# Eight weight buffers with a layout of their own each, and two raw buffers in place of three

## The chip, the cores and the metric

The kernel runs on one core of one Trainium2 chip. The metric is the device time of one execution in microseconds (us).

## The reference

One inference step of a two-layer decoder, for a prompt of 256 positions and a group of 8 x 8 new positions, together T = 320 columns. Layer 0 mixes by gated linear attention (GLA), layer 1 by a gated MLP over chunks of 128 positions (gMLP); each layer ends in a dense MLP with a squared ReLU. All is float32. Cut to what matters here:

```python
proj = x @ w_in                                  # GLA: 2048 x 6144 (and 16 columns for the gate)
o, s_fin = gla_chunked(q, k, v, log_a, s0)
h = (head_norm(o) * silu(r)) @ w_out             # 2048 x 2048
z = gelu(x @ sg_w_in + b)                        # gMLP: 2048 x 4096
h = (u * spatial(layer_norm(v))) @ sg_w_out      # 2048 x 2048
x = layer_norm(alpha * x + h)
x = layer_norm(alpha * x + square(relu(x @ w1)) @ w2)   # 2048 x 8192 and back, in each layer
```

The weights are some 390 MB, each read once; nearly all the work is these products with 320 columns.

## The kernel before

**Products.** A float32 product is made of three products of TensorE's fast type `F32R`: every operand is split into a high part (the cast to `F32R`) and a low part (what is left). `mm3` issues, for one tile of 128 x 128 weights, low weights x high activations (L161), high x low (L162) and high x high (L163), all into one PSUM tile. Activations stand as tiles of 16 rows of 320 columns (`xh`/`xl`, `yh`/`yl`, `hh`/`hl`, `oh`/`ol`); in three places rows have 322 columns (`dgh`/`dgl`).

**Units.** Weights come in units of 128 x 4 x 256 numbers (512 KB): `unit()` takes a raw buffer from the pool `wraw`, issues one transfer on SP's queue (L138), casts it on ScalarE (ACT) into a high buffer `wh` (L144), and subtracts on VectorE (DVE) into a low buffer `wl` (L145). The first unit goes in single rows and the second in pairs. `group()` then lets TensorE (PE) use the unit: two halves of 128 columns (`n`), four rows (`kk`), three matmuls each, 24 in all. The rows of the product are summed over 16 values of `k`, four units (`q`) after each other.

**Buffers.** `wraw` has three buffers. A `Ring` has four high and four low buffers of 4 x 256 numbers, 4096 bytes a partition; between the two sets stands one gap of 64 bytes, so that low buffers begin 64 bytes further in a 256-byte block than high ones. Ring a is there from the start. Ring b is added in `second_half()`, when the GLA's own tiles are given back; from then on units take turns between the rings. Activation tiles begin 128 bytes into a 256-byte block (`LINE // 2`), and a row of 320 numbers is five such blocks.

**Order.** The program is written unit by unit; a `Side` places steps of other work (gates, attention, norms) between units. The tile framework adds all waits from the use of buffers, and its scheduler sets the order on each engine from its own estimate of times, so a change of buffers can move instructions.

**Start.** The first 16 rows of x, the gate's weights (`wgr`, L293 and L296) and the first units all come over SP's queue (x rows by L225, the first two by ACT's). `low_gate()` multiplies them in 32 matmuls (`wgp`, L316 and L317).

Of the kernel before, what the change touches and what calls it, by code (L numbers as in the profile page):

```python
# [8 lines left out]
F32 = mybir.dt.float32  # L9
F32R = mybir.dt.float32r  # L10
# [5 lines left out]
P = 128  # L16
D = 2048
KT = D // P
# [12 lines left out]
UK = 4  # L31
UN = 256
NU = KT // UK
WARM = 9
LINE = 64
# [6 lines left out]
V_N = 216  # L42


class Ring:


    def __init__(self, pool, tag):
        self.pool, self.tag, self.gap = pool, tag, False

    def part(self, p, name):

        t = self.pool.tile([P, UK, UN], F32R, tag=p + self.tag, name=name)
        if not self.gap:
            self.pool.tile([P, LINE // 4], F32, tag="gap", name=name + "_gap", bufs=1)
            self.gap = True
        return t


class Side:  # L60
# [17 lines left out]
def step_kernel(ctx: ExitStack, tc: tile.TileContext, A):  # L78
    nc = tc.nc
    uid = [0]  # L80

    def nm(s):
        uid[0] += 1
        return f"{s}_{uid[0]}"
# [1 line left out]

    cp = ctx.enter_context(tc.tile_pool(name="cp", bufs=1))
    big = ctx.enter_context(tc.tile_pool(name="big", bufs=1))
    wraw = ctx.enter_context(tc.tile_pool(name="wraw", bufs=3))
    wa = ctx.enter_context(tc.tile_pool(name="wa", bufs=4))  # L90
    mm = ctx.enter_context(tc.tile_pool(name="mm", bufs=4, space=bass.MemoryType.PSUM))
    gls = ExitStack()
# [8 lines left out]
    def mmtile(n=T):  # L101

        if mx is not None:
            banks[0] = (banks[0] + 1) % 6
        return (mx if banks[0] > 3 else mm).tile([P, n], F32, tag="mm", name=nm("mm"), padded_shape=[P, 512])
# [19 lines left out]
    def col(c):  # L125
        return vec[:, c : c + 1]


    def unit(w, row0, q, col0, ring):

        raw = wraw.tile([P, UK, UN], F32, tag="raw", name=nm("raw"))
        src = w[row0 // (UK * P) + q, col0 // UN]
        hi = ring.part("h", nm("wh"))
        lo = ring.part("l", nm("wl"))
        units[0] += 1
        step = 2 if units[0] <= 2 else UK
        for k in range(0, UK, step):
            nc.sync.dma_start(raw[:, k : k + step, :], src[:, k : k + step, :])  # L138
        step = 1 if units[0] == 1 else step
        for k in range(0, UK, step):  # L140
            ks = slice(k, k + step)
            if units[0] == 1:
                before_unit(k)
            nc.scalar.copy(hi[:, ks, :], raw[:, ks, :])  # L144
            nc.vector.tensor_sub(lo[:, ks, :], raw[:, ks, :], hi[:, ks, :].bitcast(F32))  # L145
        return hi, lo

    def warm_up():

# [4 lines left out]
    def next_ring():  # L154
        turn[0] += 1
        return rings[turn[0] % len(rings)]

    def mm3(ps, wh, wl, kk, n, rh, rl, k, c0, cn, first, last):
        s = slice(n * P, (n + 1) * P)
        x_h, x_l = rh[:, k, c0 : c0 + cn], rl[:, k, c0 : c0 + cn]  # L160
        nc.tensor.matmul(ps, wl[:, kk, s], x_h, start=first, stop=False)  # L161
        nc.tensor.matmul(ps, wh[:, kk, s], x_l, start=False, stop=False)  # L162
        nc.tensor.matmul(ps, wh[:, kk, s], x_h, start=False, stop=last)  # L163

    def group(w, row0, cols, rh, rl, evict, side=None, width=T, before=None):

        ps = [mmtile(width) for _ in range(2 * len(cols))]
        for q in range(NU):
            if before is not None:
                before(q)  # L170
            for i, c in enumerate(cols):
                wh, wl = unit(w, row0, q, c, next_ring())
                for n in range(2):
                    for kk in range(UK):
                        k = q * UK + kk
                        mm3(ps[2 * i + n][:], wh, wl, kk, n, rh, rl, k, 0, width, k == 0, k == KT - 1)
                if side is not None:
                    side()
        for n in range(2 * len(cols)):
            evict(n, ps[n])  # L180
# [11 lines left out]
    lp = l2 = z = None  # L192
# [5 lines left out]
    def bigtile(tag, dt, name, width=T):  # L198

        t = (lp if tag == "b1" else big).tile([P, BIG], dt, tag=tag, name=nm(name))
        start = LINE // 2 if width == T else 0
        return t[:, start : start + KT * width].rearrange("p (k t) -> p k t", t=width)

    def parts(pair, name, width=T):
        return bigtile(pair + "0", F32R, name + "h", width), bigtile(pair + "1", F32R, name + "l", width)
# [30 lines left out]
    def before_unit(k):  # L239

        x_parts(slice(k, k + 1), first_x[k // 2][:, k % 2 : k % 2 + 1, 0:T])
# [9 lines left out]
    for c0, w in ((0, W0), (W0, W1)):  # L251
        nc.gpsimd.affine_select(out=mf[:, c0 : c0 + w], in_=mf[:, c0 : c0 + w], compare_op=ALU.is_ge, fill=0.0,
                                base=0, pattern=[[1, w]], channel_multiplier=-1)
# [89 lines left out]
    class Head:  # L343


        def __init__(hd, h):
            hd.h = h
            hd.eb, hd.ei, hd.ee = {}, {}, {}
# [140 lines left out]
        def project_kq(hd, side):  # L489

            h = hd.h

            def ev(n, ps):
                if n == 0:
                    side.flush()
                (hd.ev_k if n < 2 else hd.ev_q)(n % 2, ps)

            group(w_in, 0, (C_K + h * DK, C_Q + h * DK), xh, xl, ev, side)

        def project_v(hd, side):  # L500

            c = C_V + hd.h * DV
            hd.vb, hd.vst = {}, []

            def ev(n, ps):
                if n == 2:
                    if hd.h:
                        side.flush()
                    hd.tiles()
                    hd.gather_v(0)  # L510
                hd.ev_v(n, ps)
                if n == 3:
                    hd.gather_v(1)

            if hd.h == 0:
                group(w_in, 0, (c, c + UN), xh, xl, ev, side)
            else:
                for v0 in (0, 2):
                    group(w_in, 0, (c + v0 * P,), xh, xl, lambda n, ps, v0=v0: ev(v0 + n, ps), side)
# [175 lines left out]
    def split_o(ks):  # L695
        for k in ks:
            nc.scalar.copy(oh[:, k, 0:T], o_all[:, k, 0:T])
            nc.vector.tensor_sub(ol[:, k, 0:T], o_all[:, k, 0:T], oh[:, k, 0:T].bitcast(F32))

    def second_half():  # L700

        nonlocal lp, l2, z, gl, mx
        side.flush()
        split_o(range(4 * (H - 1), 4 * H))
        gst.close()
        gls.close()
        gl = ctx.enter_context(tc.tile_pool(name="gs", bufs=2, space=bass.MemoryType.PSUM))
        mx = ctx.enter_context(tc.tile_pool(name="mx", bufs=2, space=bass.MemoryType.PSUM))
        banks[0] = 3
        lp = ctx.enter_context(tc.tile_pool(name="lp", bufs=1))  # L710
        l2 = ctx.enter_context(tc.tile_pool(name="l2", bufs=2))
        wb = ctx.enter_context(tc.tile_pool(name="wb", bufs=4))
        rings.append(Ring(wb, "b"))
        wb.tile([P, LINE // 4], F32, tag="fill", name="fill_b", bufs=1)
        z = lp.tile([P, KT, T], F32, tag="z", name="z")
        lp.tile([P, 3 * LINE // 4], F32, tag="fill", name="fill_l")
        for q in range(2):
            nc.gpsimd.dma_start(z[:, 8 * q : 8 * q + 8, :], xT[:, 8 * q : 8 * q + 8, :])

# [194 lines left out]
    def before(q):  # L914
        if q == NU - 1:
            second_half()
        else:
            split_o(range(UK * q, UK * (q + 1)))
# [131 lines left out]
    ps = {}  # L1050
# [23 lines left out]
    for j in range(KT):  # L1074
        y, g, b = z[:, j, :], col(norm.vg + j), col(norm.vb + j)
# [4 lines left out]
        else:  # L1080
            if j not in ps:
                put_d(j)
            t = l2.tile([P, T], F32, tag="t", name=nm("t"), bufs=3)
# [70 lines left out]
```

## Time and profile before

| | |
|---|---|
| median of 2 runs | 2691.05 us (2690.93 to 2691.17) |
| profiled execution, span from the first to the last instruction | 2689.4 us |
| granted TensorE clock, mean | 1.000 |
| matmuls (PE) | 18,395, 2680.7 us busy |
| DVE / ACT / POOL busy | 1550.3 / 1162.5 / 226.4 us |
| read from memory / written | 409.60 / 22.02 MB |

The profiled execution has no time of its own beside its span; the median of the runs is 1.65 us above that span. In rows of groups, the columns are: line, engine, operation, output<-inputs, shapes, xcount | busy us, mean ns of one | idle time of the engine just before them and what ended it. In rows of the timeline they are: start us, length us, engine, line, operation. In rows of waits: who waited <- for whom: us in total, times, longest us. PEld is TensorE loading weights, SPq SP's queue of transfers. A matmul's length contains its way through the array and overlaps with the next one; the distance between two starts is what each adds to the time.

### The profile page before, as it was taken

What the parts mean: (1) busy time and instruction counts of PE and PEld (TensorE: products, weight loads), DVE (VectorE), ACT (ScalarE), POOL (GpSimd) and SP (SyncE); (2) the same over time, 40 slices, a digit from 0 to 9 for tenths busy, and PEclk for the clock granted to TensorE, in tenths of its full rate; (3) what the DMA queues carried; (4) which work ended last, traced back from release to release, by engine and by line L of the source; (5) the groups of instructions that cost most, each with busy time, mean ns of one, the idle gap of its engine ahead of it and who ended that gap; (6) DMA issues with size and microseconds to landing.
All of it is one profiled execution on the core that took longest, in us unless ns stands there. A gap on an engine that the chain in (4) does not pass through costs nothing.

```text
span 2689.4 us, 44906 instructions
## 1 busy us (share of the span) xinstructions
PE 2680.7 (100%) x18395; PEld 2658.8 (99%) x18395; DVE 1550.3 (58%) x2322; ACT 1162.5 (43%) x1638; POOL 226.4 (8%) x391
## 2 busy tenths in 40 slices
PE   9999999999999999999999999999999999999999
PEld 9999999999999999999999999999999999999998
DVE  7677677885444444444478776686444444444446
ACT  5455455564334334333446554355334333333434
POOL 4353341000000000000001032000000000000000
PEclk9999999999999999999999999999999999999999
DMA  8667667545445545444445555455445444454552
GB/s 252 220 196 249 217 198 253 189 142 159 155 150 155 151 150 156 150 153 152 150 152 161 157 158 149 134 165 153 153 150 156 150 152 154 150 155 150 152 154 79
DMA packets 138494, 442.42 MB, mean 165 GB/s; under 512 B 20912, under 2 KB 27952, under 8 KB 138288
## 3 DMA queue, kind: packets, MB, share of 16 engines
q1 hardware_dynamic: 121440, 408.08, 49.2%
q0 software_dynamic: 16304, 30.82, 3.7%
q8 instruction: 144, 2.36, 0.4%
q10 hardware_dynamic: 544, 0.66, 0.1%
q14 instruction: 62, 0.51, 0.1%
HBM read 409.60 MB, written 22.02 MB: 160 GB/s over the span
## 4 chain that ended last, share of the span: by engine, by line
PE 99%; DMA 0%; ACT 0%; DVE 0%; ACTq 0%; issue 0%; DVEq 0%
PE mm L161 32%; PE mm L163 32%; PE mm L162 31%; PE gl L631 1%; PE gl L634 1%; PE gl L589 1%; PE gl L1003 0%; PE gl L573 0%; DMA raw<-gla_w_in 0%; ACT z L1087 0%; DMA xr<-xT 0%; PE gl L558 0%; PE gl L603 0%; PE gl L574 0%; PE gl L552 0%; PE gl L1004 0%
## 5 line engine op out<-in xcount | busy, mean ns | idle before, releaser
L145 DVE TENSOR_TENSOR wl<-raw,wh 128x1024 fp32r<-128x1024 f32 (+1 forms) x740 | 902.3, 1220 | 953.2 <-ACT wh L144 950.9
L144 ACT CAST wh<-raw 128x1024 fp32r<-128x1024 f32 (+1 forms) x740 | 771.5, 1044 | 1251.9 <-PE mm L163 1127.1
L163 PE MATMUL mm<-yh,wh 128*128 128x320 f32 x2624 | 805.9, 307 | 0.0
L161 PE MATMUL mm<-yh,wl 128*128 128x320 f32 x2624 | 803.2, 309 | 0.0
L162 PE MATMUL mm<-yl,wh 128*128 128x320 f32 x2624 | 794.9, 303 | 0.0
L161 PE MATMUL mm<-hh,wl 128*128 128x320 f32 x2048 | 631.5, 308 | 0.0
L163 PE MATMUL mm<-hh,wh 128*128 128x320 f32 x2048 | 629.0, 307 | 0.0
L162 PE MATMUL mm<-hl,wh 128*128 128x320 f32 x2048 | 619.9, 303 | 0.0
L162 PEld LDWEIGHTS mm<-yl,wh 128*128 128x128 f32 x2624 | 492.7, 188 | 0.0
L163 PEld LDWEIGHTS mm<-yh,wh 128*128 128x128 f32 x2624 | 491.4, 187 | 0.0
L161 PEld LDWEIGHTS mm<-yh,wl 128*128 128x128 f32 x2624 | 491.0, 188 | 0.0
L161 PEld LDWEIGHTS mm<-hh,wl 128*128 128x128 f32 x2048 | 384.6, 188 | 0.0
L162 PEld LDWEIGHTS mm<-hl,wh 128*128 128x128 f32 x2048 | 384.6, 188 | 0.0
L163 PEld LDWEIGHTS mm<-hh,wh 128*128 128x128 f32 x2048 | 383.4, 187 | 0.0
L161 PE MATMUL mm<-xh,wl 128*128 128x320 f32 x768 | 238.2, 311 | 1.4 <-DVE wl L145 0.7
L163 PE MATMUL mm<-xh,wh 128*128 128x320 f32 x768 | 236.4, 309 | 0.0
L162 PE MATMUL mm<-xl,wh 128*128 128x320 f32 x768 | 235.2, 306 | 0.0
L161 PEld LDWEIGHTS mm<-xh,wl 128*128 128x128 f32 x768 | 144.1, 188 | 5.4 <-DVE wl L145 1.0
L162 PEld LDWEIGHTS mm<-xl,wh 128*128 128x128 f32 x768 | 144.3, 188 | 4.4 <-issue 1.2
L163 PEld LDWEIGHTS mm<-xh,wh 128*128 128x128 f32 x768 | 143.7, 187 | 2.6 <-issue 0.7
L1053 POOL CAST ident_r<-ident 128x128 fp32r<-128x128 f32 x1 | 0.3, 286 | 1027.9 <-PE gl L772 1027.9
L936 POOL DMA_DIRECT2D bsp<-sg_wT x1 | 0.6, 558 | 999.7 <-PE mm L163 999.7
(265 smaller groups left out, 2380.3 us busy)
## 6 DMA issues: line engine op xcount, KB each, us to landing
raw<-mlp_w SPq DMA_DIRECT2D x512, 512.0 KB, 3.5
raw<-gla_w_in SPq DMA_DIRECT2D x94, 512.0 KB, 4.1
raw<-sg_w_in SPq DMA_DIRECT2D x64, 512.0 KB, 3.6
st<-state SPq DMA_DIRECT2D x32, 512.0 KB, 5.7
o_state_s<-st POOLq DMA_DIRECT2D x32, 512.0 KB, 4.2
raw<-gla_w_out SPq DMA_DIRECT2D x32, 512.0 KB, 4.5
raw<-sg_w_out SPq DMA_DIRECT2D x32, 512.0 KB, 3.5
va<-blk POOLq DMA_DIRECT2D x128, 32.0 KB, 4.3
```

Of the source, the lines that this page charges most:

```text
L144: nc.scalar.copy(hi[:, ks, :], raw[:, ks, :])
L145: nc.vector.tensor_sub(lo[:, ks, :], raw[:, ks, :], hi[:, ks, :].bitcast(F32))
L161: nc.tensor.matmul(ps, wl[:, kk, s], x_h, start=first, stop=False)
L162: nc.tensor.matmul(ps, wh[:, kk, s], x_l, start=False, stop=False)
L163: nc.tensor.matmul(ps, wh[:, kk, s], x_h, start=False, stop=last)
L589: nc.tensor.matmul(pairs(pu), hd.ktp[:, kt, blk, :], hd.v_prompt(blk), start=(blk == 0), stop=(blk == 1))
L631: nc.tensor.matmul(po[:], qm[:, kt, b * P : (b + 1) * P], part[:], start=False, stop=(b == DB - 1 and kt == 1 and part is sth))
L634: nc.tensor.matmul(pairs(pu), kz[:, i, kt, g, :], hd.v_sample(g), start=True, stop=True)
L936: nc.gpsimd.dma_start(wsT, A["sg_wT"])
L1053: nc.gpsimd.tensor_copy(ident_r[:], ident[:])
```

## The change

A class `Weights` maps row `k` of a unit to its place in a buffer: `base + k // 2 * a + k % 2 * b`. Buffers grow by 256 bytes to 4352, seventeen blocks of 256, and the gap between the sets goes, so that all buffers begin on a block. A table `PLACES` gives each of a ring's four turns a place for high and one for low weights and an order of rows, 1 or -1. `Q` is 64 bytes, `UN` one row of 1024 bytes:

- ring a, turn 0: rows as before, low 64 bytes further in the block than high; turn 1: each row 64 bytes further than the one before it; turn 2: the same places, with `kk` running from 3 to 0; turn 3: rows stand in the order 0, 2, 1, 3, rows 1 and 3 shifted by 128 bytes.
- ring b: rows as before; high and low begin at 0 and 0, 0 and 128, 128 and 192, 64 and 0 bytes in the block.

The sixteen longer buffers take 4096 bytes more in all, as much as the third raw buffer, which goes. Casts and subtractions write rows in pairs with steps `a` and `b`. The first matmul of a sum is now the first in the unit's order of rows.

```diff
+class Weights:
+    def row(self, k):
+        return self.base + k // 2 * self.a + k % 2 * self.b
+    def put(self, ks):
+        k, n = ks.start, ks.stop - ks.start
+        if n == 1:
+            return self.tile[:, self.row(k) : self.row(k) + UN].rearrange("p (a b n) -> p a b n", a=1, b=1)
+        one = self.tile[:, self.row(k) : self.row(k) + 1]
+        return bass.AP(tensor=one.tensor, offset=one.offset,
+                       ap=[list(one.ap[0]), [self.a, n // 2], [self.b, 2], [1, UN]])
...
+Q = LINE // 4
+PLACES = {
+    "a": [((0, 2 * UN, UN), (Q, 2 * UN, UN), 1),
+          ((0, 2 * UN + 2 * Q, UN + Q), (Q, 2 * UN + 2 * Q, UN + Q), 1),
+          ((0, 2 * UN + 2 * Q, UN + Q), (Q, 2 * UN + 2 * Q, UN + Q), -1),
+          ((0, UN, 2 * UN + 2 * Q), (Q, UN, 2 * UN + 2 * Q), 1)],
+    "b": [((0, 2 * UN, UN), (0, 2 * UN, UN), 1),
+          ((0, 2 * UN, UN), (2 * Q, 2 * UN, UN), 1),
+          ((2 * Q, 2 * UN, UN), (3 * Q, 2 * UN, UN), 1),
+          ((Q, 2 * UN, UN), (0, 2 * UN, UN), 1)],
+}
 class Ring:
-        self.pool, self.tag, self.gap = pool, tag, False
-    def part(self, p, name):
-        t = self.pool.tile([P, UK, UN], F32R, tag=p + self.tag, name=name)
...
+    def parts(self, hi, lo):
+        *at, order = PLACES[self.tag][self.turn % 4]
+        self.turn += 1
+        h, l = (Weights(self.pool.tile([P, UK * UN + LINE], F32R, tag=p + self.tag, name=n), *x)
+                for p, n, x in zip("hl", (hi, lo), at))
+        return h, l, order
...
-    wraw = ctx.enter_context(tc.tile_pool(name="wraw", bufs=3))
+    wraw = ctx.enter_context(tc.tile_pool(name="wraw", bufs=2))
...
-            nc.scalar.copy(hi[:, ks, :], raw[:, ks, :])
-            nc.vector.tensor_sub(lo[:, ks, :], raw[:, ks, :], hi[:, ks, :].bitcast(F32))
-        return hi, lo
+            src = raw[:, ks, :].rearrange("p (a b) n -> p a b n", b=min(step, 2))
+            nc.scalar.copy(hi.put(ks), src)
+            nc.vector.tensor_sub(lo.put(ks), src, hi.put(ks).bitcast(F32))
+        return hi, lo, range(UK)[::order]
...
-                    for kk in range(UK):
+                    for kk in order:
...
-                        mm3(ps[2 * i + n][:], wh, wl, kk, n, rh, rl, k, 0, width, k == 0, k == KT - 1)
+                        mm3(ps[2 * i + n][:], wh, wl, kk, n, rh, rl, k, 0, width,
+                            q == 0 and kk == order[0], q == NU - 1 and kk == order[-1])
```

The order changes most where the program starts. On SP's queue, before, from the first transfers on (`raw` are units of weights, `xr` rows of x, `wgr` the gate's weights):

```order
L138 DMA raw_155<-gla_w_in 128x512 x2
L138 DMA raw_201<-gla_w_in 128x512 x2
L225 DMA xr_234<-xT 128x2x320
L225 DMA xr_236<-xT 128x2x320
L138 DMA raw_242<-gla_w_in 128x1024
L293 DMA wgr<-gla_w_low 128x256
L225 DMA xr_302<-xT 128x2x320
L138 DMA raw_272<-gla_w_in 128x1024
```

The same place on SP's queue after the change:

```order
L172 DMA raw_155<-gla_w_in 128x512 x2
L172 DMA raw_200<-gla_w_in 128x512 x2
L261 DMA xr_233<-xT 128x2x320
L261 DMA xr_235<-xT 128x2x320
L329 DMA wgr<-gla_w_low 128x256
L332 DMA wgr_340<-gla_w_gate 16x1024
L261 DMA xr_301<-xT 128x2x320
L172 DMA raw_241<-gla_w_in 128x1024
```

The third unit's transfer (`raw_242`, now `raw_241`) has moved behind three others: its buffer is now the first unit's.

On ACT, before, from the second unit's cast on (`wh` high weights, `xh` high part of x, `wgp` the gate's weights):

```order
L144 CAST wh_202<-raw_201 128x512 x2
L230 CAST xh_89<-xr_234 128x640
L230 CAST xh_89<-xr_236 128x640
L144 CAST wh_243<-raw_242 128x1024
L230 CAST xh_89<-xr_302 128x640
L144 CAST wh_273<-raw_272 128x1024
L230 CAST xh_89<-xr_304 128x640
L310 CAST wgp_418<-wgr 128x8x3x16
```

The same place on ACT after the change:

```order
L179 CAST wh_201<-raw_200 128x2x256 x2
L266 CAST xh_89<-xr_233 128x640
L266 CAST xh_89<-xr_235 128x640
L266 CAST xh_89<-xr_301 128x640
L179 CAST wh_242<-raw_241 128x4x256
L266 CAST xh_89<-xr_303 128x640
L346 CAST wgp_417<-wgr 128x8x3x16
L179 CAST wh_272<-raw_271 128x2x2x256
```

The third unit's cast stands behind one more cast of x and the fourth's behind the gate's weights, and the casts write four rows with steps of their own (`128x2x2x256`, or `128x4x256` where the steps are equal) in place of one run of 1024. On PE, gate matmuls (`wgp`) stand between the third and fourth and the fourth and fifth units; before, the first sixteen followed the fourth unit.

More of the change, by code (lines that the diff above doesn't have):

```diff
@@ L42, with __init__, __getitem__ @@
 V_N = 216
+class Weights:
+    def __init__(self, tile, base, a, b):
+        self.tile, self.base, self.a, self.b = tile, base, a, b
+    def row(self, k):
[7 more added lines that the diff above has]
+                       ap=[list(one.ap[0]), [self.a, n // 2], [self.b, 2], [1, UN]])
+    def __getitem__(self, at):
+        p, k, c = at
+        return self.tile[p, self.row(k) + c.start : self.row(k) + c.stop]
+Q = LINE // 4
[9 more added lines that the diff above has]
+}
 class Ring:
     def __init__(self, pool, tag):
-        self.pool, self.tag, self.gap = pool, tag, False
-    def part(self, p, name):
-        t = self.pool.tile([P, UK, UN], F32R, tag=p + self.tag, name=name)
[L54 to L57, printed above, removed]
+        self.pool, self.tag, self.turn = pool, tag, 0
+    def parts(self, hi, lo):
[4 more added lines that the diff above has]
+        return h, l, order
 class Side:
@@ L132, in unit @@
         src = w[row0 // (UK * P) + q, col0 // UN]
-        hi = ring.part("h", nm("wh"))
-        lo = ring.part("l", nm("wl"))
+        hi, lo, order = ring.parts(nm("wh"), nm("wl"))
         units[0] += 1
@@ L171, in group @@
             for i, c in enumerate(cols):
-                wh, wl = unit(w, row0, q, c, next_ring())
+                wh, wl, order = unit(w, row0, q, c, next_ring())
                 for n in range(2):
-                    for kk in range(UK):
+                    for kk in order:
                         k = q * UK + kk
-                        mm3(ps[2 * i + n][:], wh, wl, kk, n, rh, rl, k, 0, width, k == 0, k == KT - 1)
+                        mm3(ps[2 * i + n][:], wh, wl, kk, n, rh, rl, k, 0, width,
+                            q == 0 and kk == order[0], q == NU - 1 and kk == order[-1])
                 if side is not None:
@@ L715, in second_half @@
         z = lp.tile([P, KT, T], F32, tag="z", name="z")
-        lp.tile([P, 3 * LINE // 4], F32, tag="fill", name="fill_l")
+        lp.tile([P, LINE], F32, tag="fill", name="fill_l")
         for q in range(2):
```

## The prediction

> **What bounds the kernel now.** I began with the page's shares of busy time and its chain, because the change touches TensorE's weights, the two engines that make them and the transfers that feed those, and only one of these can set the end.
>
> ```profile
> PE 2680.7 (100%) x18395; PEld 2658.8 (99%) x18395; DVE 1550.3 (58%) x2322; ACT 1162.5 (43%) x1638; POOL 226.4 (8%) x391
> PEclk9999999999999999999999999999999999999999
> PE 99%; DMA 0%; ACT 0%; DVE 0%; ACTq 0%; issue 0%; DVEq 0%
> PE mm L161 32%; PE mm L163 32%; PE mm L162 31%; PE gl L631 1%; PE gl L634 1%; PE gl L589 1%; PE gl L1003 0%; PE gl L573 0%; DMA raw<-gla_w_in 0%; ACT z L1087 0%; DMA xr<-xT 0%; PE gl L558 0%; PE gl L603 0%; PE gl L574 0%; PE gl L552 0%; PE gl L1004 0%
> ```
>
> TensorE is never without work, its clock is full in every slice, and 99% of the chain is matmuls, nearly all from the three lines of `mm3`. So two things count: how far apart one matmul starts after the other, and whether TensorE ever has to wait for weights. A matmul's recorded length tells neither, since matmuls overlap. I therefore read start times. This is one unit of weights (24 matmuls) in the first MLP, from the timeline of PE; the columns are start, length, engine, line:
>
> ```profile
> 1149.73 0.31 PE L161 MATMUL mm<-hh,wl 128*128 128x320 f32 x1
> 1149.88 0.30 PE L162 MATMUL mm<-hl,wh 128*128 128x320 f32 x1
> 1150.02 0.31 PE L163 MATMUL mm<-hh,wh 128*128 128x320 f32 x1
> 1150.17 0.31 PE L161 MATMUL mm<-hh,wl 128*128 128x320 f32 x1
> ...
> 1153.20 0.31 PE L161 MATMUL mm<-hh,wl 128*128 128x320 f32 x1
> ```
>
> From 1149.73 to 1153.20 there are 24 starts: 3.47 us a unit, **0.1446 us a matmul**. Within a triple the steps are not alike: 0.15 after the first, 0.14 after the second, 0.15 after the third. Same shape, same engine, full clock, so something other than the arithmetic adds to some of them.
>
> Here the rows carry a tile's place in memory. The activation rows are 320 columns, 1280 bytes, five whole blocks of 256; a weight row is 1024 bytes, four blocks; the low weights stand 64 bytes further in their block than the high ones. So before the change every matmul of `mm3` of this width meets the same places. Two stretches have other places:
>
> ```profile
> 545.16 0.30 PE L161 MATMUL mm<-dgh,wl 128*128 128x322 f32 x1
> 545.31 0.31 PE L162 MATMUL mm<-dgl,wh 128*128 128x322 f32 x1
> ...
> 573.52 0.31 PE L163 MATMUL mm<-dgh,wh 128*128 128x322 f32 x1
> 573.68 0.31 PE L161 MATMUL mm<-dgh,wl 128*128 128x322 f32 x1
> ...
> 574.12 0.31 PE L161 MATMUL mm<-yh,wl 128*128 128x320 f32 x1
> L161 PE MATMUL mm<-dgh,wl 128*128 128x322 f32 x192 | 59.6, 311 | 0.0
> L163 PE MATMUL mm<-dgh,wh 128*128 128x322 f32 x192 | 59.6, 310 | 0.0
> L162 PE MATMUL mm<-dgl,wh 128*128 128x322 f32 x192 | 59.4, 309 | 0.0
> ```
>
> ```profile
> 2676.31 0.31 PE L1084 MATMUL mm<-nl,ident_r 128*128 128x320 f32 x1
> ...
> 2677.93 0.31 PE L1085 MATMUL mm<-nh,ident_r 128*128 128x320 f32 x1
> ```
>
> In the first, activation rows are 322 wide, so each row starts 8 bytes further in its block. The three groups hold 192 matmuls a line in three such stretches, so one stretch is 192, and four others of the trace stand among them: 28.96 us for 196, 0.1478 each, or 0.1468 when scaled by 320/322. Single steps there reach 0.16 (573.52 to 573.68). In the second, one stationary tile is loaded again and again: 1.62 us for 11 steps, 0.1473. **So places cost something, and two stretches with other places than the kernel's are both slower, by 0.0022 and 0.0027 us a matmul.**
>
> **The matmuls after the change.** The lines of `mm3` have 5,888 matmuls each (2,624 + 2,048 + 768 + 256 + 192 by group), 17,664 together. Of eight buffers one, the first of ring a, keeps today's places; the units go round the buffers evenly, so 7/8, 15,456 matmuls, get new ones: rows shifted by 64 bytes from one to the next, the same with the four rows taken backwards, rows alternating by 128, and in ring b low and high at equal places, 128 apart, or 64 apart elsewhere in the block. None of these stands in the trace. Bounds from its rows: if each step were the shortest one seen (0.140, rounded as 1149.88 to 1150.02), 15,456 x -0.0046 = -71 us; if each were as in the stretch of 322 columns, 15,456 x 0.0022 = +34 us; as in the last stretch, 15,456 x 0.0027 = +42 us; the single steps of 0.16 are no mean of anything, and I leave them out. I take +0.0016, two thirds of the way to the two slow stretches, since these include offsets of 8 bytes that the new layouts lack: **+25 us**. It lies nearest to the 322-column row, the only one with many places.
>
> The Trainium skill, SBUF — State Buffer, section "Who interferes with whom", gives TensorE two independent read ports, one for the moving operand and one for the weights, and says that it waits for nobody. By that, places would be worth nothing and this term would be 0; the trace's unequal steps of one shape speak against it, and the sum above does not use it.
>
> **The weights' supply with two raw buffers.** In steady state, each transfer is issued by SP when VectorE has finished with the raw buffer it overwrites:
>
> ```profile
> 1117.65 7.26 SPq L138 DMA_DIRECT2D raw<-mlp_w  x3
> 1116.40 1.22 DVE L145 TENSOR_TENSOR wl<-raw,wh 128x1024 fp32r<-128x1024 f32 x1 [0.64 <-ACT wh L144]
> 1118.78 1.05 ACT L144 CAST wh<-raw 128x1024 fp32r<-128x1024 f32 x1 [2.41 <-PE mm L163]
> 1125.71 1.05 ACT L144 CAST wh<-raw 128x1024 fp32r<-128x1024 f32 x1 [2.41 <-PE mm L163]
> raw<-mlp_w SPq DMA_DIRECT2D x512, 512.0 KB, 3.5
> SPq L138 <- DVE wl L145: 2150.6, 692, 8.9
> ACT wh L144 <- PE mm L163: 1127.1, 514, 3.8
> ```
>
> The subtraction ends at 1117.62, the transfer starts at 1117.65 and lands after 3.5, and its cast comes at 1125.71, having waited for TensorE to free a weight buffer, as 514 casts do. With two buffers the transfer for the cast at 1125.71 starts after the subtraction that follows the cast at 1118.78: 1118.78 + 1.05 + 0.03 + 1.22 + 0.03 = 1121.11, landing at 1124.61, still 1.1 us early. So steady state loses nothing. Casts and subtractions now write four separate rows. The nearest rows of that kind are the first unit's single rows, quoted with the start below: 0.71 for two casts, 0.76 for two subtractions. Between no change and the price of four single ones, a cast costs up to 4 x 0.36 - 1.05 = 0.4 us more and a subtraction up to 4 x 0.38 - 1.22 = 0.3. I take 0: one instruction with a longer pattern is nearer to one long instruction than to four. ACT is busy for 43% and DVE for 58%, so TensorE covers it either way; the 1.1 us of the loop would shrink to 0.4. If that cover too is gone, a unit is late by the rest, first drawn from the stock of ready buffers (eight, or four in the mixer's first projections).
>
> At the start there is no cover. The rows are the chain and ACT, DVE and SP at that time:
>
> ```profile
> 4.97 6.32 DMA raw<-gla_w_in
> 11.31 1.07 ACT wh L144
> 12.40 1.24 DVE wl L145
> 13.68 0.42 PE mm L161
> 4.31 0.71 ACT L144 CAST wh<-raw 128x256 fp32r<-128x256 f32 x2 [1.22 <-DMA raw<-gla_w_in]
> 6.28 0.76 DVE L145 TENSOR_TENSOR wl<-raw,wh 128x256 fp32r<-128x256 f32 x2
> 7.06 0.33 SPq L138 DMA_DIRECT2D raw<-gla_w_in  x1
> 14.25 1.05 ACT L144 CAST wh<-raw 128x1024 fp32r<-128x1024 f32 x1 [0.98 <-DMA raw<-gla_w_in]
> raw<-gla_w_in SPq DMA_DIRECT2D x94, 512.0 KB, 4.1
> st<-state SPq DMA_DIRECT2D x32, 512.0 KB, 5.7
> ```
>
> The third unit's transfer goes out at 4.97 into a third buffer, and TensorE waits for it. With two it waits for the first unit's last subtraction, which ends at 7.04, the time at which the fourth goes out today (7.06, cast at 14.25). So the third cast moves from 11.31 to about 14.25: **+2.9 us**. Behind it, units come at half the loop: (6.3 + 1.06 + 1.23) / 2 = 4.3 us while transfers take 6.3, against 3.47 of matmuls; the thirteen gate matmuls that the new order puts ahead of the fourth and fifth unit (13 x 0.147 = 1.9 us) fill part of that. I add 2 us, between 0 and (4.3 - 3.47) x 8 units = 7. What is queued on SP behind a waiting raw transfer waits too: the gate weights, the x rows and later the state loads; their readers are the side steps, which TensorE runs between units.
>
> The accumulation flags now follow the order of the rows and cost nothing.
>
> **Sum:** the profiled execution's span 2689.4 + 25 + 2.9 + 2 = 2719.3. The median of the runs, 2691.05, lies 1.65 above that span, so the time is **2721 us**, +1.1%. The bound for telling it from no change is about 2% (54 us).
>
> **Rivals.**
> - *Places do not matter, or the seven cancel.* For it: one old layout out of many may be typical. Against: unequal steps in the rows. The layout term is 0: 2691 + 5 = 2696. This is also where the skill's rule of separate ports leads.
> - *The new places are faster (the other side).* Before the change one step in three is short. If the new places give two short ones, a triple loses 0.007 us: 15,456 / 3 x -0.007 = -36 us, with the start 2660. It decides as soon as the seven together save more than the start's 5 us, a mean step under 0.1443. For it: 0.14 does occur in the rows; against: neither stretch with other places has a mean under 0.1468.
> - *Two raw buffers starve the mixer's part.* There the median landing is 4.1, and with a state load's 5.7 the loop is (5.7 + 1.05 + 1.22) / 2 = 4.0 us, 0.5 over 3.47. For half of its 94 units that is 25 us on top: 2746. Against: half the loop at 4.1 is 3.2, under 3.47.
>
> **How the numbers follow.** Forecast 0.60 (2700 to 2745), no effect of places 0.14, faster places 0.14, starvation 0.12. The range 2686 to 2752 takes in the two slow stretches' 34 and 42 us with the start's 10 and the starvation's 2746 above, and no effect or a small saving below; it leaves out most of the faster case and the end of the others. Over 2% faster (under 2637) needs nearly the whole -71: 0.03. Over 2% slower (above 2745): 0.12. Within: 0.85.
>
> **What would show it.** Starts of one unit's 24 matmuls, buffer by buffer: the buffer with the old places keeps 3.47 us, the others differ, each the same every time it comes round; ring b's first, with low and high alike, should be about 3.53, as with the one tile loaded again and again. TensorE's third unit should start near 16.6 instead of 13.7, and later waits of TensorE should stay at nothing. The forecast is wrong if units with new places run under 3.46 on average, or if the casts' waits turn from TensorE to transfers and TensorE shows gaps.

## The result, and the profile after

The changed kernel takes **2724.74 us** (median of 2 runs, 2724.38 to 2725.11), against 2691.05: 33.7 us more, a ratio of 1.0125 with a 95% interval from 1.0095 to 1.0154. The forecast was 2721 with a range of 2686 to 2752. The profiled execution has a span of 2722.7, 33.3 us over that of before.

The page of the changed kernel, its busy times, clock, chain and two groups of supply instructions:

```profile
PE 2705.7 (99%) x18395; PEld 2680.9 (98%) x18395; DVE 1550.4 (57%) x2322; ACT 1161.1 (43%) x1638; POOL 226.7 (8%) x391
PEclk9999999999999999999999999999999999999999
PE 78%; DVE 3%; DMA 3%; ACT 1%; issue 0%; ACTq 0%; POOL 0%; DVEq 0%; POOLq 0%
L180 DVE TENSOR_TENSOR wl<-raw,wh 128x1024 fp32r<-128x1024 f32 (+1 forms) x740 | 901.1, 1218 | 986.2 <-ACT wh L179 984.3
L179 ACT CAST wh<-raw 128x1024 fp32r<-128x1024 f32 (+1 forms) x740 | 771.7, 1043 | 1280.2 <-PE mm L198 997.4
```

The matmuls are as many and the clock is full. But the chain is no longer TensorE alone: transfers, casts and subtractions enter it with some 7% of the span. The fall of TensorE's share from 99% to 78% is mostly another thing: the profile could follow this chain back only to 421.85 us, so its shares add up to 85% and not to 100%. The casts and subtractions themselves cost what they did, 1043 and 1218 ns now, 1044 and 1220 before, although ring a's turns 1 to 3 now write four separate rows.

**Where the units' time went.** The starts of units in the same MLP as in the prediction, from the timeline of PE of the changed kernel (start, length, engine, line), one row for the first matmul of a unit; units alternate between ring b and ring a:

```profile
1155.40 0.31 PE L196 MATMUL mm<-hh,wl 128*128 128x320 f32 x1
...
1158.92 0.31 PE L196 MATMUL mm<-hh,wl 128*128 128x320 f32 x1
...
1162.39 0.31 PE L196 MATMUL mm<-hh,wl 128*128 128x320 f32 x1
...
1165.89 0.31 PE L196 MATMUL mm<-hh,wl 128*128 128x320 f32 x1
...
1169.38 0.31 PE L196 MATMUL mm<-hh,wl 128*128 128x320 f32 x1
...
1172.90 0.31 PE L196 MATMUL mm<-hh,wl 128*128 128x320 f32 x1
...
1176.39 0.31 PE L196 MATMUL mm<-hh,wl 128*128 128x320 f32 x1
...
1179.91 0.31 PE L196 MATMUL mm<-hh,wl 128*128 128x320 f32 x1
...
1183.41 0.31 PE L196 MATMUL mm<-hh,wl 128*128 128x320 f32 x1
```

The distances are 3.52 (ring b, 128 and 192), 3.47 (ring a, the old place), 3.50 (b, 64 and 0), 3.49 (a, rows shifted by 64 each), 3.52 (b, 0 and 0), 3.49 (a, the same backwards), 3.52 (b, 0 and 128) and 3.50 (a, rows shifted by 128). The round of eight takes 28.01 us, where eight old units take 27.73 (1146.27 to 1174.00 in the timeline of before). The old place keeps its 3.47, and all seven others are slower, each by 0.02 to 0.05 us every time it comes round. Of the 736 units (17,664 / 24) the first 102 know ring a alone, whose four places are 0.02 us above the old one on average. So the units give 634 x 0.28 / 8 + 102 x 0.02 = 24 us. Over the whole trace, the mean step between the starts of neighbouring `mm3` matmuls, leaving out steps from 0.2 us on, went from 144.66 to 145.93 ns: 17,664 x 1.27 ns = **22.4 us**.

**The rest is waits.** These are the rows of PE's and ACT's waits after (waiter <- for whom: us in total, times, longest):

```profile
PE mm L196 <- DVE wl L180: 3.6, 2, 3.2
PE mm L196 <- DVE nw L223: 2.3, 1, 2.3
...
PE mm L197 <- DVE yl L858: 1.0, 1, 1.0
...
ACT wh L179 <- PE mm L198: 997.4, 440, 4.9
ACT wh L179 <- DMA raw<-mlp_w: 113.0, 67, 5.6
```

Before, casts waited 24.4 us for `mlp_w`, as its rows of waits have it:

```profile
ACT wh L144 <- DMA raw<-mlp_w: 24.4, 12, 3.7
```

So some casts did turn from waiting for TensorE to waiting for transfers, and TensorE has gaps. I add up what each distance between neighbouring matmul starts above 0.31 us has over a normal step of 0.147, by stretch of the span:

| us lost in gaps | 0–20 | 20–445 | 445–560 | 560–620 | 620 to the end | all |
|---|---|---|---|---|---|---|
| before | 1.9 | 11.6 | 0.2 | 0.0 | 0.4 | 14.1 |
| after | 4.2 | 15.4 | 3.3 | 1.2 | 0.4 | 24.5 |
| `before_raw2` (below) | 3.6 | 15.9 | 2.2 | 5.5 | 0.4 | 27.6 |
| `old_places` (below) | 3.4 | 15.5 | 2.9 | 4.1 | 0.4 | 26.3 |
| `halves4` (below) | 1.8 | 14.2 | 1.8 | 0.0 | 0.4 | 18.2 |

After minus before is **10.4 us**. With the 22.4 of the places this makes 32.8 of the 33.3 us between the spans. Nothing more is lost in the dense MLP of layer 0 and after it, beyond 620 us, which is more than three quarters of the span.

### The profile page after: what moved, and what is told of

Same layout as the page of the kernel before. It is cut to its first block, busy times and chain, and to the rows that moved or that the text cites. A ratio compares the mean times of both kernels' runs of the same rounds, so it can differ in the third digit from the quotient of the medians.

```text
span 2722.7 us, 44866 instructions
## 1 busy us (share of the span) xinstructions
PE 2705.7 (99%) x18395; PEld 2680.9 (98%) x18395; DVE 1550.4 (57%) x2322; ACT 1161.1 (43%) x1638; POOL 226.7 (8%) x391
## 4 chain that ended last, share of the span: by engine, by line
PE 78%; DVE 3%; DMA 3%; ACT 1%; issue 0%; ACTq 0%; POOL 0%; DVEq 0%; POOLq 0%
PE mm L196 26%; PE mm L198 26%; PE mm L197 26%; DMA raw<-gla_w_out 2%; DVE wl L180 1%; ACT wh L179 1%; DMA raw<-mlp_w 1%; DMA z<-xT 0%; PE gl L1039 0%; ACT z L1123 0%; DMA o_state_s<-st 0%; DVE t L853 0%; DVE dgl L813 0%; DVE t L852 0%; DVE yl L858 0%
## 5 line engine op out<-in xcount | busy, mean ns | idle before, releaser
L180 DVE TENSOR_TENSOR wl<-raw,wh 128x1024 fp32r<-128x1024 f32 (+1 forms) x740 | 901.1, 1218 | 986.2 <-ACT wh L179 984.3
L179 ACT CAST wh<-raw 128x1024 fp32r<-128x1024 f32 (+1 forms) x740 | 771.7, 1043 | 1280.2 <-PE mm L198 997.4
L197 PE MATMUL mm<-yl,wh 128*128 128x320 f32 x2624 | 804.5, 307 | 1.0 <-DVE yl L858 1.0
L197 PE MATMUL mm<-hl,wh 128*128 128x320 f32 x2048 | 628.0, 307 | 0.0
```

Of the source, the lines that this page charges most:

```text
L179: nc.scalar.copy(hi.put(ks), src)
L180: nc.vector.tensor_sub(lo.put(ks), src, hi.put(ks).bitcast(F32))
```

## The experiments

After the result I held three theories. **A**: the places cost some 23 us and the smaller raw pool some 10. **B**: the raw pool costs nearly all of it, and the places next to nothing. **C**: the places cost nothing by themselves, but TensorE pays for going from one layout to another. In text and tables, "high" and "low" places are bytes into a 256-byte block; in diffs they are float32 numbers, `Q` being 16 of them.

**`old_places`**: all eight buffers of the changed kernel get the old place; two raw buffers stay.

```diff
-PLACES = {
...
-}
+PLACES = {t: 4 * [((0, 2 * UN, UN), (Q, 2 * UN, UN), 1)] for t in "ab"}
```

> The changed kernel with all eight rows of the table of places set to the old place (low weights 64 bytes further in the block than high, rows 1024 bytes apart, order 1); two raw buffers and the writing in rows stay. Theory A (places cost some 23 us, the two raw buffers and the moved order some 10): about 2701 us, a unit's 24 matmuls back at 3.47 us, the gaps of the changed kernel's start and at 463 us still there. Theory B (the raw buffers cost nearly all): about 2720 us. Theory C (it is the switching between places from unit to unit that costs, not the places): as A here, 2701 us.

**`before_raw2`**: the kernel before with two raw buffers and nothing else.

```diff
-    wraw = ctx.enter_context(tc.tile_pool(name="wraw", bufs=3))
+    wraw = ctx.enter_context(tc.tile_pool(name="wraw", bufs=2))
```

> The kernel before with two raw buffers in place of three and nothing else. Theories A and C: about 2700 us, TensorE waiting at the start (third unit 2.4 us late) and where the attention part ends. Theory B: 2715 us or more. If casts and subtractions that write separate rows cost something, this is faster than the changed kernel with the old places.

Measured: `old_places` 2708.15 us, ratio 1.0063 (1.0046 to 1.0080); `before_raw2` 2709.38, ratio 1.0066 (1.0051 to 1.0081). The raw pool alone costs 17 to 18 us, more than A's 10 and less than B's 24 to 30; the new places then cost the changed kernel only 16.6 us on top. The two kernels agree although one writes longer buffers with the new class and the other does not, so the class and the padding cost nothing that shows beside a spread of some 4 us within either. The waits of `before_raw2` show the same places as those of the changed kernel:

```profile
PE mm L162 <- DVE yl L822: 2.8, 3, 1.3
PE mm L161 <- DVE wl L145: 2.4, 1, 2.4
...
PE mm L161 <- DVE nw L187: 1.5, 1, 1.5
```

They are the third unit (`wl`), the attention's last norm (`nw`) and the entry to the first MLP (`yl`). The 12.2 us of gaps that `old_places` has over before don't fill its 16.3 us of span. Some 4 more lie in steps between 0.15 and 0.31 us behind the waits (excess over 0.147 us: 30.4 us against 25.9). Most of them are two stretches of 3.4 us, from 16.99 and from 597.25 us on, in which its granted clock is 0.50; a step then takes about 0.27 us, and each stretch loses half its length, 3.4 us together. Before and the changed kernel have no such stretch in their profiles before the last matmuls.

That raw pool and places, 17 and 22 us, make 33.7 together and not 39 comes mostly from two things: the changed kernel lacks the 3.4 us at half clock, and has 10.4 us of gaps in place of 12.2. Why it has fewer was not tested apart. That slower matmuls give the supply more time per unit would fit, and the stretch from 560 to 620 us, 1.2 against 4.1 and 5.5, points that way.

**`gap0`**: the kernel before, three raw buffers, with the 64-byte gap moved behind both sets, so that high and low weights stand at equal places.

```diff
-        if not self.gap:
+        if p == "l" and not self.gap:
```

> The kernel before, three raw buffers, with the 64-byte gap moved behind both sets of buffers, so that high and low weights begin at equal places in the block, and nothing else. Theory A: every matmul of 320 columns at the pace of ring b's first buffer in the changed kernel, 0.1466 us, so (0.1466 - 0.1445) x 17,100 = 36 us more, 2727 us. Theories B and C: no change, 2691 us.

Measured: 2727.25 us (2727.1 to 2727.36), ratio 1.0134 (1.0119 to 1.0149). **A alone gives this number.** Nothing but 64 bytes has moved: same instructions, the same three raw buffers, one layout throughout. Its gaps sum to 14.0 us, as before. The timeline of PE has 24 matmuls in 3.52 us, where before took 3.47 (1149.73 to 1153.20 in the prediction's rows):

```profile
1151.41 0.31 PE L161 MATMUL mm<-hh,wl 128*128 128x320 f32 x1
...
1154.93 0.31 PE L161 MATMUL mm<-hh,wl 128*128 128x320 f32 x1
```

Rows rounded to 0.01 us are too coarse for single steps. Over the whole trace the mean steps after the three matmuls of a triple are equal, 146.7 ns each; before they are 147.5, 140.6 and 145.9. Mean step 146.72 ns: 17,664 x 2.06 = 36.4 us, and 36.1 were measured. B and C both fall as sole causes.

**`scan16`**: each of the sixteen products of the two MLPs that have 32 units has one pair of places in all buffers, no rows shifted; two raw buffers.

```diff
+def places(unit):
+    if 128 <= unit < 384:
+        n = (unit - 128) // 32
...
+    high, low = n % 4, (n % 4 + n // 4) % 4
+    return (high * Q, 2 * UN, UN), (low * Q, 2 * UN, UN), 1
...
-        *at, order = PLACES[self.tag][self.turn % 4]
-        self.turn += 1
+        *at, order = places(unit)
```

> The changed kernel with one place for all buffers in each of the sixteen products of the two MLPs (32 units each): high weights at 0, 64, 128 or 192 bytes in the block, low weights 0, 64, 128 or 192 bytes further; the rest has the old place. Theory A: the time of 24 matmuls differs from product to product, 3.47 us where the old place stands (second MLP product 5 of 16 in the order), 3.5 to 3.56 in most others, and perhaps under 3.47 in some. Theory C: all sixteen near 3.47 us, since no unit differs from its neighbours. Theory B says nothing on it but expects 3.47 as well.

Measured: 2731.87 us in a single run. What counts is the time of three matmuls by pair of places (ns, the sum of the three mean steps, from steps under 0.2 us; the first eight units of an MLP, whose rows have 322 columns, are left out):

| high \ low | 0 | 64 | 128 | 192 |
|---|---|---|---|---|
| 0 | 440.1 | **433.4** | 439.6 | 446.6 |
| 64 | 437.8 | 440.0 | 435.6 | 436.7 |
| 128 | **433.4** | 438.7 | 440.0 | 440.0 |
| 192 | 440.0 | 436.7 | 440.0 | 440.0 |

Two pairs share the lowest value; one is the kernel's old place. The worst shows in the timeline of PE as a unit of 3.58 us:

```profile
2272.20 0.32 PE L194 MATMUL mm<-yh,wl 128*128 128x320 f32 x1
...
2275.78 0.32 PE L194 MATMUL mm<-yh,wl 128*128 128x320 f32 x1
```

Equal places are 440 four times out of four, wherever in the block they stand.

**`alternate`**: does going from one layout to another cost anything? Two places only, the two at 433.4. While there is only ring a they change at every unit, later at every second one.

```diff
-PLACES = {
...
-}
+OLD, ALT = ((0, 2 * UN, UN), (Q, 2 * UN, UN), 1), ((2 * Q, 2 * UN, UN), (0, 2 * UN, UN), 1)
+PLACES = {"a": [OLD, ALT, OLD, ALT], "b": [ALT, OLD, ALT, OLD]}
```

> Two raw buffers, and only two places in place of eight, by turns from unit to unit: the old one (high 0, low 64 bytes into the block) and high 128, low 0. In the scan of sixteen places each of these two, alone, took 433.4 ns for three matmuls. Theory P (a place has its price whatever stands before and behind it): 2708 us, as with the old place everywhere, 433.4 ns for three. Theory S (the change from one place to the next costs something too, since the old place took 436.8 ns among the seven others of the change): 3.4 ns x 5,810 triples = 20 us more, 2728.

Measured: 2708.20 us, ratio 1.0065 (1.0048 to 1.0082), the time of `old_places` within the spread of the runs (2706.57 to 2711.78 here); theory S asked for 20 us more. Theory P holds for these two. Unit starts of it, from the timeline of PE; the place changes at 1157.35, and the next unit, to 1160.82, takes 3.47 again:

```profile
1153.88 0.31 PE L188 MATMUL mm<-hh,wl 128*128 128x320 f32 x1
...
1157.35 0.31 PE L188 MATMUL mm<-hh,wl 128*128 128x320 f32 x1
```

The 436.8 ns on which the expectation built theory S was my own misreading: that mean had taken in steps with waits. Without steps from 0.2 us on, the old place has 434.0 ns in the changed kernel, and 3.47 us a unit in the rows above.

**`scan_rows`**: the same scan with finer offsets and with shifted rows, ring a's three kinds among them.

```diff
+R, E = 2 * UN, UN
...
+    ((0, R, E), (8, R, E), 1),
+    ((0, R, E), (24, R, E), 1),
+    ((8, R, E), (24, R, E), 1),
...
+    ((0, R + 2 * Q, E + Q), (3 * (E + Q), -R - 2 * Q, -E - Q), 1),
+    ((0, R, E), (0, R + 2 * Q, E + Q), 1),
+    ((0, E, R + 2 * Q), (Q, R, E), 1),
+    ((0, E, R + 2 * Q), (2 * Q, E, R + 2 * Q), 1),
```

> Two raw buffers; each of the sixteen MLP products of 32 units has one layout of its own in all buffers, the rest the old one. The layouts are low weights 32, 96 or 16 bytes behind the high ones, both shifted by 16, 32 or 96 bytes, and the three shifts from row to row that ring a has in the change (64 bytes a row, the same backwards, 128 bytes by turns), high and low shifted together, apart, or one alone. Theory P: a triple's time follows from the places alone, so each of the layouts with shifted rows has one steady mean, between the 433.4 and 446.6 ns of the layouts without shift; none under 433.4; total about 2725 to 2735 us. Rival: 433.4 ns isn't the least, and some layout takes 420 (three steps of 140) or 427: a kernel with it everywhere would save 17,664 / 3 x 6.7 to 13.4 ns = 39 to 79 us.

Measured: 2730.62 us in a single run. Three matmuls take, in ns, reckoned as above: 440.0 with low 32, 96 or 16 bytes behind high; 442.2 to 443.4 with both at odd multiples of 16 or 32 bytes; ring a's shifted rows 436.5, the same backwards 436.7, rows by turns of 128 bytes 436.7; high and low shifted alike 438.3, in opposite directions 440.0, low alone 440.0, high alone by 128 bytes 438.4, both by turns 128 apart 436.7. The old place has 434.3 in this run. A unit with high at 32 and low at 96:

```profile
916.27 0.31 PE L212 MATMUL mm<-hh,wl 128*128 128x320 f32 x1
...
919.82 0.31 PE L212 MATMUL mm<-hh,wl 128*128 128x320 f32 x1
```

3.55 us, though low is 64 bytes behind high here as in the old place: the place in the block counts too, not the distance alone. The rival, something under 433.4, did not come up in 30 layouts. The eight layouts' prices, taken one by one from the two scans, predict the changed kernel: 433.4 + 436.5 + 436.7 + 436.7 + 440.1 + 439.6 + 440.0 + 437.8 = 3500.8 ns, times the eight triples of a unit 28.01 us for a round, which is the round in its trace. Their mean, 437.6, is 4.2 above the old place, and the mean of ring a's four 2.4. So the whole kernel should lose (634 x 4.2 + 102 x 2.4) x 8 ns = 23 us, against 22.4 measured. Prices of places, added up, are the whole of that term; nothing is left for C.

**`raw1`**: how heavy is the loop of one raw buffer? The kernel before with `bufs=1`.

> The kernel before with one raw buffer in place of three. If a raw buffer goes through transfer, cast and subtraction before its next transfer (3.5 + 1.06 + 1.24 = 5.8 us), this loop sets the pace for all 736 units: 736 x 5.8 = 4270 us. With two buffers half of that, 2.9 us, stands against 3.47 us of matmuls, so steady state loses nothing. Rival (the subtraction isn't what the transfer waits for, or part of the loop overlaps): between 2750 and 3900 us, and two buffers then have more to spare than 0.57 us a unit.

Measured: 4611.05 us in a single run. The loop does set the pace, and it is longer than I put it. From the timeline of DVE:

```profile
1492.26 1.23 DVE L145 TENSOR_TENSOR wl<-raw,wh 128x1024 fp32r<-128x1024 f32 x1 [4.75 <-ACT wh L144]
1498.34 1.23 DVE L145 TENSOR_TENSOR wl<-raw,wh 128x1024 fp32r<-128x1024 f32 x1 [4.85 <-ACT wh L144]
1504.39 1.23 DVE L145 TENSOR_TENSOR wl<-raw,wh 128x1024 fp32r<-128x1024 f32 x1 [4.83 <-ACT wh L144]
```

6.05 to 6.08 us from one to the next, against 5.8 expected; the whole span, 4609.3 / 736, gives 6.26. Half of 6.08 is 3.04, under the 3.47 of a unit's matmuls: two buffers keep up while nothing else delays a cast, with 0.4 us a unit to spare, and no more.

**`halves4` and `halves6`**: raw buffers of two rows, four of them (the memory of two whole ones) or six (the memory of three); old places. The first, with `bufs=4`:

```diff
-    wraw = ctx.enter_context(tc.tile_pool(name="wraw", bufs=3))
+    wraw = ctx.enter_context(tc.tile_pool(name="wraw", bufs=4))
...
-        raw = wraw.tile([P, UK, UN], F32, tag="raw", name=nm("raw"))
...
+        raws = []
+        for k in range(0, UK, 2):
+            raws.append(wraw.tile([P, 2, UN], F32, tag="raw", name=nm("raw")))
+            nc.sync.dma_start(raws[-1][:], src[:, k : k + 2, :])
...
+            raw = raws[k // 2][:, k % 2 : k % 2 + step, :]
...
-            nc.scalar.copy(hi[:, ks, :], raw[:, ks, :])
...
+            nc.scalar.copy(hi[:, ks, :], raw)
```

> The kernel before, with its old places, but raw buffers of two rows (256 KB) in place of four, and four of them: as much memory as two whole ones. Every unit is now two transfers, two casts, two subtractions. Theory G (the 17 us that two raw buffers cost with the old places come from the grain: a whole buffer is held through transfer, cast and subtraction, 5.8 us, though its first half is free earlier): the third unit's first half can go after the first unit's second row, nearly 1 us sooner, and a half's loop is some 1.9 + 0.6 + 0.65 = 3.1 us, a quarter of it 0.8 against 1.73 us of matmuls; most of the waits go, 2692 to 2698 us. Theory M (they come from the memory: two buffers' bytes in flight are too few where transfers take 4 to 6 us): 2705 to 2712, or more, since transfers are shorter and more in number.

> The same with six raw buffers of two rows, as much memory as the kernel before has. Theory G and theory M alike: no waits that the kernel before lacks, 2691 us; if finer pieces bring the third unit's cast forward from 11.31 us, up to 2 us less. Rival: twice as many transfers on SP's queue cost more than they bring, or the casts, now 0.57 twice in place of 1.05, come late beside the other work of ACT and DVE: 2693 to 2705.

Measured: `halves4` 2693.39 us, ratio 1.0009 (0.9999 to 1.0018); `halves6` 2691.95, ratio 1.0003 (0.9993 to 1.0012). **Theory G holds: with the bytes of two raw buffers, 16 of the 18 us are gone.** One size in the expectation was off. The issues of `halves4` and its waits:

```profile
raw<-mlp_w SPq DMA_DIRECT2D x1024, 256.0 KB, 2.7
```

```profile
ACT wh L145 <- DMA raw<-mlp_w: 26.8, 25, 4.6
```

Half a transfer lands after 2.7 us, not 1.9, where a whole one took 3.5; but the casts' waits for `mlp_w` fall to 26.8 us, about as before, from the 103.7 of `before_raw2`:

```profile
ACT wh L144 <- DMA raw<-mlp_w: 103.7, 64, 5.0
```

No version beats the kernel before: its place is the shortest of the 30 tried (one other is equal), and finer raw buffers bring no time, only 4096 bytes a partition.

## Why the prediction was right, point by point

- **Places, +25 us forecast.** Measured 22.4 by the steps, or 0.00145 us for each of 15,456 matmuls, where 0.0016 was taken. (The units do not quite go round evenly: with the first 102 on ring a alone, some 15,150 matmuls have a new place.) The choice "two thirds of the way to the two slow stretches" came near since all seven new layouts lie between the short triple (433.4 ns) and the equal steps (440), some of them at 440 itself. But no row had priced one of them, so that places cost something was read from the trace, and that it was two thirds was in part luck. The single prediction of ring b's first buffer, 3.53, came out as 3.52, and the old place kept 3.47. The Trainium skill, SBUF — State Buffer, section "Who interferes with whom", gives TensorE two independent read ports and says that it never waits on anyone. The prediction's reading of it as 0 for this term does not hold here: in `gap0` 64 bytes cost 36 us.
- **Start, +2.9 us.** The mechanism was right: SP sends the third unit's transfer at 7.20, just after the first unit's last subtraction. From the timeline of the changed kernel:

```profile
13.89 1.04 ACT L179 CAST wh<-raw 128x1024 fp32r<-128x1024 f32 x1 [1.12 <-DMA raw<-gla_w_in]
...
14.97 1.23 DVE L180 TENSOR_TENSOR wl<-raw,wh 128x1024 fp32r<-128x1024 f32 x1 [0.15 <-ACT wh L179]
...
16.25 0.42 PE L196 MATMUL mm<-xh,wl 128*128 128x320 f32 x1 [3.18 <-DVE wl L180]
```

  The third cast starts at 13.89 (forecast 14.25, before 11.31) and TensorE's third unit at 16.25 (forecast 16.6, before 13.68): 2.6 us. The gaps from 20 to 445 us grew by 3.8; they hold the 2 us that were put behind the start, and whatever the mixer's supply cost.
- **Steady state, 0.** Right where it was worked out: beyond 620 us there are no gaps that the kernel before lacks, and casts in separate rows cost nothing more (the prediction gives such rows to all units; it is three of the eight places). **"Later waits of TensorE should stay at nothing" was wrong**: 3.1 us at the end of the attention and 1.2 at the entry to the first MLP. With it came, in part, what the prediction had named as a sign of being wrong: casts wait more for transfers (113.0 us for `mlp_w` in place of 24.4), and TensorE shows gaps. The step that failed is the cover of 1.1 us in the raw loop, read from one calm place of an MLP. This is the changed kernel there, in order of time: first ACT's timeline, then the chain (start, us, what), then two transfers from SP's timeline:

```profile
449.93 1.05 ACT L179 CAST wh<-raw 128x1024 fp32r<-128x1024 f32 x1 [3.61 <-PE gl L667]
456.54 1.05 ACT L179 CAST wh<-raw 128x1024 fp32r<-128x1024 f32 x1 [2.10 <-DMA raw<-gla_w_out]
461.31 2.17 ACT L179 CAST wh<-raw 128x1024 fp32r<-128x1024 f32 x2 [3.40 <-DVE o_all L573]
463.50 1.28 ACT L222 ACT_TABLE_LOAD   x1
464.80 0.53 ACT L222 ACTIVATE ny<-gl,eps_h 128x320 f32<-128x320 f32 x1
```

```profile
444.92 4.93 DMA raw<-gla_w_out
...
451.00 1.24 DVE wl L180
452.26 4.26 DMA raw<-gla_w_out
...
457.62 1.24 DVE wl L180
458.88 3.54 DMA raw<-gla_w_out
```

```profile
449.52 0.33 SPq L172 DMA_DIRECT2D raw<-gla_w_out  x1
...
463.64 0.33 SPq L172 DMA_DIRECT2D raw<-gla_w_out  x1
```

  In the chain one raw buffer goes round alone: transfers into it start at 444.92, 452.26 and 458.88, that is 6.6 to 7.3 us a unit against 3.47 of matmuls. (ACT's timeline puts the 3.61 us before the cast at 449.93 down to TensorE, but the transfer for that cast lands at 444.92 + 4.93 = 449.85.) The other raw buffer is filled by the transfer of 449.52, but its cast comes only at 461.31: ACT has stood for 3.40 us until DVE was done with `o_all`, attention work. So that buffer is held, and the next transfer into it starts at 463.64, 14 us after the one before. By the kernel this should be the first cast into ring b, which takes over memory of the GLA's own tiles; the profile doesn't name the buffer.

  What is queued on ACT behind these casts, the table load and `ny` of the norm, is late too. TensorE waits 2.33 us for that norm to be done with its PSUM tile, not for weights. So with two raw buffers one cast that is held up leaves a single buffer to carry the supply. Pieces of half the size take most of it away (`halves4`: 0.2 us of gaps from 445 to 480, and 1.6 more at 497.81, before a matmul of a norm).
- **The rivals.** "Places do not matter" fell with `gap0`. "The new places are faster" fell with the unit rows and the two scans: none of the seven is. "Two raw buffers starve the mixer's part" came true at a small part of its price: at most those 3.8 us, where 25 were worked out, and 4.3 at the hand-overs that it did not name.
- **The sum.** 25 + 2.9 + 2 against 22.4 + 10.4: the places 2.6 us too high, the waits 5.5 too low. That the errors partly cancel, so that the total comes within 4 us, is in part luck.

## What to carry to other kernels

When an engine is busy for 99% and one shape shows two step lengths, read starts, not lengths, and ask what differs between the steps; a run with one layout per product prices many layouts at once, and prices found one by one added up to the mixture here. Size a pool of raw buffers by its whole loop (transfer, cast, subtraction, 6.05 us here) and by the places where the engine that releases them is held up by other work, not by one calm stretch. If memory is short, cut the buffers smaller before taking one away.

## What the runs showed that I had not expected

- The step between two matmuls of 320 columns at full clock depends on where low and high weights stand in 256-byte blocks, down to 16 bytes (both shifted by 16, 443.4 ns): from 433.4 to 446.6 ns for three, that is 3%, and 36 us of this kernel for 64 bytes moved. The activations were not moved in any run, and why one place costs more than another the runs don't show.
- After some waits TensorE's granted clock is halved for a while. In `raw1`, with a mean granted clock of 0.898, the timeline of PE after a wait of 2.31 us has the first five of these rows. The last is the same stretch by windows: its length, busy us and instructions of PE, PEld, DVE, ACT and POOL, then the granted clock (0.50), the busy share of the DMA engines and GB/s:

```profile
1505.67 0.64 PE L161 MATMUL mm<-hh,wl 128*128 128x320 f32 x1 [2.31 <-DVE wl L145]
...
1508.24 0.47 PE L161 MATMUL mm<-hh,wl 128*128 128x320 f32 x1
1508.51 0.47 PE L162 MATMUL mm<-hl,wh 128*128 128x320 f32 x1
...
1509.03 0.31 PE L161 MATMUL mm<-hh,wl 128*128 128x320 f32 x1
1509.18 0.31 PE L162 MATMUL mm<-hl,wh 128*128 128x320 f32 x1
```

```profile
1505.60:1509.00 3.40, 3.33 (x12) 3.33 (x13) 0.02 (x1) 0.00 (x0) 0.00 (x0) 0.50 0.50 152
```

  Twelve steps take 3.36 us (1505.67 to 1509.03), most of them 0.27, then it is 0.15 again. So that wait cost 2.3 us and 1.6 more (3.36 - 12 x 0.147). The two such stretches of `old_places` follow waits of 2.38 and 1.26 us, while the changed kernel's wait of 2.33 us before 465.90 is followed by steps of 0.15; what decides it the runs don't show.
